# A ring of their own for the fp32 experts' weights, and one pair of PSUM banks for an fp32 step

## The chip, the core and the metric

The kernel runs on one core of a Trainium2 chip. The time is in device microseconds of one execution, as the median of several runs; lower is better. Durations in the profile come from one profiled execution.

## What is computed

One layer of a diffusion transformer on 1024 tokens of width 1024: a mixer of two kinds of attention, and behind it a mixture of experts. All tensors are fp32. The change touches the experts alone:

```python
logits = (h @ w_router + b_router).astype(jnp.float32)
top_logits, top_e = lax.top_k(logits, TOP_K)          # 4 of 32 experts for each token
top_w = jax.nn.softmax(top_logits, axis=-1).astype(h.dtype)
...
def expert_block(args):
    xe, e = args
    gu = xe @ w_gu[e] + b_gu[e]                       # 1024 -> 2048
    x_glu = jnp.minimum(gu[:, :D_FF], SWIGLU_LIMIT)
    x_lin = jnp.clip(gu[:, D_FF:], -SWIGLU_LIMIT, SWIGLU_LIMIT)
    act = (x_lin + 1) * (x_glu * jax.nn.sigmoid(SWIGLU_ALPHA * x_glu))
    return act @ w_dn[e] + b_dn[e]                    # 1024 -> 1024
```

Each token's result is the sum of its four experts' outputs, weighted by `top_w`. The weights of all 32 experts, 12 MB each, have to be read once.

## The kernel before

The phases ahead of the experts (mixer, router, slot tables) end near 1150 us of the profile. `moe` then works through the 32 experts, ordered by their number of tokens: expert of rank r gets `CAPS[r]` slots, 304 for the first and 56 for the last; tokens beyond that go to an overflow part. By its slots an expert has one of three modes:

- T (16 experts, 136 to 304 slots): weights are the stationary operand, tokens the moving one, the result is transposed. Products run in fp32r on a split: a weight piece `raw` of 128 x 1024 becomes `hi` (a rounded copy, ScalarE, L1518) and `lo` (`raw - hi`, VectorE, L1529). TensorE adds `hi` times both halves of the tokens (L1701) and `lo` times the upper half (L1702); above 256 slots there are three products (L1704 to L1706).
- N (9 experts, 128 slots): tokens are stationary, the same split of weights (L1669 to L1671).
- F (7 experts, 56 to 96 slots): plain fp32 products from `raw`, without a split (L1698). Each matmul uses 64 columns of the array; the two halves `a = 0, 64` write the two halves of the partitions.

The places p = 0 to 31 alternate: even places hold the T experts from the widest on, places 1 to 13 the F experts, and odd places from 15 on the N experts. An expert has six steps: four of kind U (j = 0 to 3, a quarter of gate and up columns each) and two of kind D (half of the output columns each). A step takes four pieces (q = 0 to 3), each with two of the eight blocks of the contraction. The list `steps` alternates the two experts of a pair step by step, so T and F (later T and N) steps follow each other all along.

The order on each engine is written out by the program, in the order in which Python issues the instructions. Within a step, `tra` (T and F) or `nat` (N) issues the matmuls of a quarter and then calls `slot(p)`. A slot advances the generators in `chains` (the work that follows a step: activation functions, splits of activations, and from `hot` and `cold` the transposes of tokens, which are started in T and N slots only), then issues up to two splits and up to two loads of later pieces. There is one ring of 8 `raw` pieces for all modes, 7 `hi` and 6 `lo`. A split is not issued until its load is three slots old. The raw buffer of an F piece comes free when TensorE has read it, that of another piece when VectorE has made its `lo`. All weight loads are issued by SP, one after the other (L1497): one that waits for its buffer holds back those behind it.

PSUM has a ring of three tiles `g5`, each of two banks (`gps`, 3 buffers). A T step or an F step takes two of them (`pss` in `tra`, one for each half `gi`), an N step one. They are emptied after the step: in a wide U step by ScalarE's bias (L1762) and VectorE's add (L1768), in a wide D step by L1836 and L1845, in F steps and the two widest T by VectorE's L1776 (U) and ScalarE's L1836 (D). `evac` issues ScalarE's part at the end of q = 3, the chain issues VectorE's part in the slot at the end of the step, behind the splits of the slots before.

Of the kernel before, what the change touches and what calls it, by code (L numbers as in the profile page):

```python
# [18 lines left out]
P = 128  # L19
# [1420 lines left out]
class Moe2(Tail):  # L1440
    def moe(self):
# [6 lines left out]
        N_HI, N_LO, N_RAW = 7, 6, 8  # L1448
# [4 lines left out]
        lop = self.pool(es, "lo5", N_LO)  # L1453
        es = ExitStack()
# [29 lines left out]
        st = {"l": 0, "h": 0, "s": 0, "out": 0, "c": 0, "n": -9}  # L1484
        at = {}
        whole = lambda i: mode[pieces[i][1]] == "F"

        def load(n=1, eng="sync"):
            for _ in range(n):
                o = st["l"] - N_RAW  # L1490
                if st["l"] >= len(pieces) or o >= st["c"] and whole(o):
                    return
                k, p, j, q = pieces[st["l"]]
                e = ereg(eng, p)
                r = rawp.tile([P, 1024], F32, name="raw5")
                src = A["w_gu" if k == "U" else "w_dn"]
                getattr(nc, eng).dma_start(r, src[ds(e, 1), j * 4 + q].rearrange("a p c -> p (a c)"))  # L1497
                if whole(st["l"]):
                    his[pieces[st["l"]]] = r
                else:  # L1500
                    raws[st["l"]] = r
                at[st["l"]] = st["n"]
                st["l"] += 1

        def split_hi(n=1, now=False):
            for _ in range(n):
                while st["h"] < len(pieces) and whole(st["h"]):
                    st["h"] += 1
                i = st["h"]
                if i >= len(pieces):  # L1510
                    return
                if i >= st["l"]:
                    load(i + 1 - st["l"])
                if i >= st["l"] or at[i] > st["n"] - 3 > -3 and not now:
                    return
                st["out"] += 1
                his[pieces[i]] = hi = hip.tile([P, 1024], F32R, name="hi5")
                ACT.activation(hi, raws[i], AF.Copy)  # L1518
                st["h"] += 1

        def split_lo(n=1):
            for _ in range(n):
                while st["s"] < len(pieces) and whole(st["s"]):
                    st["s"] += 1
# [3 lines left out]
                los[pieces[i]] = lo = lop.tile([P, 1024], F32R, name="lo5")  # L1528
# [149 lines left out]
        def tra(key, x, p, evac):  # L1678
# [6 lines left out]
            for q in range(4):  # L1685
# [26 lines left out]
                if q < 3:  # L1712
                    slot(p)
# [391 lines left out]
```

## Time and profile before

| | |
|---|---|
| median of 3 runs | 2846.4 us (2839.77 to 2849.7) |
| profiled execution | 2844.65 us, span 2842.8 us |
| first T matmul of an expert, first F step, first N step | 1182, 1211, 1978 us |
| last matmul of an expert | 2799 us |
| PE busy over the span | 2646.8 us (93%) |
| DVE, ACT busy | 1747.6 us (61%), 1409.9 us (50%) |
| splits | 600 `hi` at 1052 ns, 600 `lo` at 1222 ns |
| weight loads of the experts | 768 of 512 KB |

The part to look at lies between 1182 and 2799 us. A group of instructions is named by its line, engine, tiles (out<-in) and count; behind the bar stand its busy time, the mean of one, and the idle time of the engine just before it with what ended it. "PE g L1698 <- DVE gx L1768" says that a matmul of line 1698 that writes a tile `g` waited until the VectorE instruction of line 1768 was done. Matmuls are pipelined and their ends are modelled, so the length of a step is read from its start to the start of the next.

### The profile page before, as it was taken

How to read it: one execution, taken by the hardware profiler on the slowest of the kernel's cores; microseconds unless marked ns; L12 is line 12 of the kernel's file. 1: busy time of each engine (PE TensorE's matmuls, PEld its weight loads, DVE VectorE, ACT ScalarE, POOL GpSimd, SP SyncE). 2: the span in 40 equal slices, each digit the busy share in tenths (PEclk: the TensorE clock that was granted, in tenths of full speed). 3: DMA queues.
4: the chain of work that ended last, by engine and by line, in shares of the span. 5: the costliest groups of instructions: out<-in, count | busy, mean ns of one | idle time of the engine just before them, and what ended most of it. 6: DMA issues, size and time to landing. Idle time of an engine off the chain costs nothing. (4 is left out here: it accounts for less than half of the span.)

```text
span 2842.8 us, 52306 instructions
## 1 busy us (share of the span) xinstructions
PE 2646.8 (93%) x19986; PEld 2251.9 (79%) x19986; DVE 1747.6 (61%) x3001; ACT 1409.9 (50%) x2334; POOL 557.1 (20%) x485
## 2 busy tenths in 40 slices
PE   6999999999999999599988999999999999999993
PEld 3788887555688778599978888998889888988883
DVE  3722322767788456454454554555888888888885
ACT  3421212555677235334334444445676777777774
POOL 2310001656543313201011011011001100110001
PEclk8999999999999999699999999999999999999997
DMA  6224551502232443567687687787889888998886
GB/s 234 72 94 176 185 196 45 159 23 41 49 73 48 156 150 113 195 209 252 230 268 251 239 281 249 258 290 262 279 288 306 289 283 298 311 307 281 301 300 235
DMA packets 197422, 588.15 MB, mean 207 GB/s; under 512 B 50400, under 2 KB 57136, under 8 KB 197024
## 3 DMA queue, kind: packets, MB, share of 16 engines
q1 hardware_dynamic: 174432, 521.51, 53.5%
q0 software_dynamic: 19152, 61.86, 8.2%
q8 instruction: 158, 2.59, 0.4%
q10 hardware_dynamic: 3584, 1.40, 0.2%
q14 instruction: 96, 0.79, 0.1%
HBM read 527.92 MB, written 58.08 MB: 206 GB/s over the span
## 5 line engine op out<-in xcount | busy, mean ns | idle before, releaser
L1529 DVE TENSOR_TENSOR lo<-raw,hi 128x1024 fp32r<-128x1024 f32 x600 | 722.4, 1222 | 405.6 <-ACT hi L1518 395.6
L1518 ACT ACTIVATE hi<-raw 128x1024 fp32r<-128x1024 f32 x600 | 611.0, 1052 | 59.8 <-DMA raw<-in_w_gu_dram 40.5
L1701 PE MATMUL g<-xT,hi 128*128 128x320 f32 (+10 forms) x1792 | 524.3, 334 | 10.6 <-DVE gx L1776 7.7
L1702 PE MATMUL g<-xT,lo 128*128 128x256 f32 x1792 | 483.5, 280 | 0.0
L1701 PEld LDWEIGHTS g<-xT,hi 128*128 128x128 f32 x1792 | 337.1, 188 | 26.6 <-issue 10.2
L1702 PEld LDWEIGHTS g<-xT,lo 128*128 128x128 f32 x1792 | 337.6, 188 | 1.5
L1870 POOL DMA_INDIRECT f_d<-y,slot x34 | 55.3, 1627 | 1252.8 <-ACT y L1858 1127.1
L1701 PE MATMUL g<-aT,hi 128*128 128x288 f32 (+10 forms) x896 | 264.9, 336 | 4.8 <-DVE gx L1776 4.8
L1702 PE MATMUL g<-aT,lo 128*128 128x256 f32 x896 | 242.4, 281 | 0.0
L1701 PEld LDWEIGHTS g<-aT,hi 128*128 128x128 f32 x896 | 169.1, 189 | 12.0 <-issue 6.1
L174 DVE TENSOR_TENSOR wlo<-raw,whi 128x1024 fp32r<-128x1024 f32 x33 | 42.1, 1289 | 219.4 <-ACT whi L173 219.2
L1702 PEld LDWEIGHTS g<-aT,lo 128*128 128x128 f32 x896 | 169.4, 189 | 0.4
L1698 PE MATMUL g<-xN,raw 128*64 128x88 f32 (+5 forms) x3584 | 136.1, 237 | 20.8 <-DVE gx L1768 12.2
L1698 PEld LDWEIGHTS g<-xN,raw 128*64 128x64 f32 x3584 | 129.8, 140 | 27.7 <-DVE gx L1768 13.0
L859 ACT ACTIVATE p<-S 128x512 f32<-128x512 f32 x160 | 94.2, 596 | 103.8 <-PE S L858 99.0
L613 DVE TENSOR_REDUCE mn<-S 128x1 f32<-128x512 f32 x180 | 100.8, 594 | 66.3 <-PE S L612 66.0
L400 PE MATMUL mm<-hTh,whi 128*128 128x512 f32 (+1 forms) x416 | 123.9, 385 | 1.7 <-ACT whi L173 1.7
L400 PE MATMUL mm<-hTh,wlo 128*128 128x512 f32 (+1 forms) x416 | 123.2, 384 | 0.0
L400 PE MATMUL mm<-hTl,whi 128*128 128x512 f32 (+1 forms) x416 | 123.1, 383 | 0.0
L1669 PE MATMUL g<-hi,xN 128*128 128x512 f32 x288 | 117.5, 408 | 0.0
L1671 PE MATMUL g<-lo,xN 128*128 128x512 f32 x288 | 113.7, 395 | 0.0
L1670 PE MATMUL g<-hi,xN 128*128 128x512 f32 x288 | 113.7, 395 | 0.0
(415 smaller groups left out, 5735.4 us busy)
## 6 DMA issues: line engine op xcount, KB each, us to landing
raw<-in_w_gu_dram SPq DMA_DIRECT2D x512, 512.0 KB, 5.9
raw<-in_w_dn_dram SPq DMA_DIRECT2D x256, 512.0 KB, 4.6
raw<-in_w_mod_dram SPq DMA_DIRECT2D x40, 512.0 KB, 4.3
raw<-in_w_in_dram SPq DMA_DIRECT2D x34, 512.0 KB, 4.7
x<-in_x_dram SPq DMA_DIRECT2D x16, 512.0 KB, 5.0
sig_d<-stg POOLq DMA_DIRECT2D x16, 512.0 KB, 2.9
sig<-sig_d SPq DMA_DIRECT2D x8, 1024.0 KB, 4.9
kraw<-ka_d SPq DMA_DIRECT2D x16, 320.0 KB, 6.9
```

The source lines that it names most:

```text
L400: T.matmul(ps[:, :n], w[:, ks], h[:, k, a:a + n], start=k == 0 and pi == 0, stop=k == KT - 1 and pi == 2)
L613: nc.vector.tensor_reduce(out=u.mn[:, i, j:j + 1], in_=ps[:, :n], op=ALU.min, axis=AX.X)
L859: nc.scalar.activation(u.p[t // 2][:, t % 2 * 512:t % 2 * 512 + 512], ps, AF.Exp, scale=-1.0)
L1518: ACT.activation(hi, raws[i], AF.Copy)
L1529: V.tensor_tensor(out=lo, in0=raws.pop(i), in1=f(his[pieces[i]]), op=ALU.subtract)
L1669: T.matmul(ps[:m], x[:, kk, P:P + m], hi[:, cs], start=False, stop=False)
L1670: T.matmul(ps[:m], x[:, kk, :m], hi[:, cs], start=False, stop=False)
L1671: T.matmul(ps[:m], x[:, kk, :m], lo[:, cs], start=False, stop=kk == 7)
L1698: T.matmul(ps[a:a + 64, :c], hi[:, cs.start + a:cs.start + a + 64], x[:, kk, :], start=first, stop=last)
L1701: T.matmul(ps[:, :2 * c], hi[:, cs], x[:, kk, :], start=first, stop=False)
L1702: T.matmul(ps[:, :256], lo[:, cs], x[:, kk, :256], start=False, stop=last)
L1870: G.indirect_dma_start(out=self.f_d, out_offset=bass.IndirectOffsetOnAxis(ap=SL[p][xi][:n, 0:1], axis=0), in_=Y[p][xi][:n], in_offset=None ...
```

## The change

Five things change in `moe`.

1. F pieces get a ring of their own, `rawf`, of four buffers, one step's worth. `load_whole` fills it: a new function `few` calls it after each piece's last use in an F step, so a step's four pieces are loaded in the second half of the F step before. The ring of the others shrinks from 8 to 6 `raw`, 7 to 6 `hi`, 6 to 5 `lo`; the sum stays 21 pieces.
2. `few` takes the place of `tra` for F. It takes one PSUM tile (two banks, each with two parts of 256 columns) instead of two, and runs over the four pieces twice: r = 0 and r = 1 for the two parts of a bank. The count of matmuls is the same.
3. Slots of F steps advance chains but issue no split and no load. In slots of T and N steps both splits go ahead while fewer than five pieces are split beyond the ones used (`st["c"]` counts pieces of T and N only). The rule of three slots and `ready` are gone.
4. `load` takes T and N pieces only, up to six beyond the last `lo`.
5. When the last F step is done, the four buffers of `rawf` become two more `hi` and two more `lo`; the limit rises to eight `hi` and seven `lo`.

At the end of the program two of the eight loads of the residual go to `hi` buffers instead of `raw` ones.

On TensorE, the third F step of place 9 (88 slots) and the T step D of place 8 after it. `g5` are PSUM tiles, `raw5` and `rawf` weight pieces. Before:

```order
L1702 MATMUL g5_16071<-xT_14947,lo5_15975 128x256
L1698 MATMUL g5_16182<-xN_15461,raw5_15997 64x88 x8
L1698 MATMUL g5_16183<-xN_15461,raw5_15997 64x88 x8
L1698 MATMUL g5_16182<-xN_15461,raw5_16017 64x88 x8
L1698 MATMUL g5_16183<-xN_15461,raw5_16017 64x88 x8
L1698 MATMUL g5_16182<-xN_15461,raw5_16036 64x88 x8
L1698 MATMUL g5_16183<-xN_15461,raw5_16036 64x88 x8
L1698 MATMUL g5_16182<-xN_15461,raw5_16062 64x88 x8
L1698 MATMUL g5_16183<-xN_15461,raw5_16062 64x88 x8
L1701 MATMUL g5_16275<-aT_15462,hi5_16126 128x432
L1702 MATMUL g5_16275<-aT_15462,lo5_16128 128x256
```

and now:

```order
L1693 MATMUL g5_16060<-xT_14948,lo5_15937 128x256
L1717 MATMUL g5_16177<-xN_15453,rawf_16018 64x88 x8
L1717 MATMUL g5_16177<-xN_15453,rawf_16028 64x88 x8
L1717 MATMUL g5_16177<-xN_15453,rawf_16039 64x88 x8
L1717 MATMUL g5_16177<-xN_15453,rawf_16049 64x88 x8
L1717 MATMUL g5_16177<-xN_15453,rawf_16018 64x88 x8
L1717 MATMUL g5_16177<-xN_15453,rawf_16028 64x88 x8
L1717 MATMUL g5_16177<-xN_15453,rawf_16039 64x88 x8
L1717 MATMUL g5_16177<-xN_15453,rawf_16049 64x88 x8
L1692 MATMUL g5_16263<-aT_15454,hi5_15967 128x432
L1693 MATMUL g5_16263<-aT_15454,lo5_15969 128x256
```

Eight rows of eight matmuls as before. The two tiles have become one, and each piece is read twice, four groups apart.

On VectorE around the end of the T step before this F step (its PSUM tiles are read by the two adds into `gx` that are 2x216 wide). Before:

```order
L1786 SCALAR_TENSOR_TENSOR aN_15785<-gx_16055,gs_16088 128x2x88
L1529 TENSOR_TENSOR lo5_16128<-raw5_16064,hi5_16126 128x1024
L1529 TENSOR_TENSOR lo5_16132<-raw5_16066,hi5_16130 128x1024
L1768 TENSOR_TENSOR gx_16142<-g5_16070,gx_16142 128x2x216
L1770 TENSOR_SCALAR gx_16142<-gx_16142 128x2x216
L1768 TENSOR_TENSOR gx_16153<-g5_16071,gx_16153 128x2x216
L1772 TENSOR_SCALAR gx_16153<-gx_16153 128x2x216
L1529 TENSOR_TENSOR lo5_16162<-raw5_16068,hi5_16160 128x1024
L1529 TENSOR_TENSOR lo5_16166<-raw5_16090,hi5_16164 128x1024
L1784 TENSOR_TENSOR gs_16200<-gs_16200,gx_16142 128x2x216
L1786 SCALAR_TENSOR_TENSOR gx_16142<-gx_16153,gs_16200 128x2x216
L1793 TENSOR_TENSOR aT_15462<-gx_16142,aT_15462 128x2x216
```

and now:

```order
L1532 TENSOR_TENSOR lo5_16105<-raw5_15780,hi5_16103 128x1024
L1532 TENSOR_TENSOR lo5_16127<-raw5_15893,hi5_16125 128x1024
L1779 TENSOR_TENSOR gx_16139<-g5_16059,gx_16139 128x2x216
L1781 TENSOR_SCALAR gx_16139<-gx_16139 128x2x216
L1779 TENSOR_TENSOR gx_16150<-g5_16060,gx_16150 128x2x216
L1783 TENSOR_SCALAR gx_16150<-gx_16150 128x2x216
L1532 TENSOR_TENSOR lo5_16159<-raw5_15917,hi5_16157 128x1024
L1795 TENSOR_TENSOR gs_16194<-gs_16194,gx_16139 128x2x216
L1797 SCALAR_TENSOR_TENSOR gx_16139<-gx_16150,gs_16194 128x2x216
L1804 TENSOR_TENSOR aT_15454<-gx_16139,aT_15454 128x2x216
L1787 TENSOR_SCALAR gx_16255<-g5_16177,bcol_14223 128x88 x2
L1787 TENSOR_SCALAR gx_16256<-g5_16177,bcol_14223 128x88 x2
```

Before, two splits `lo` stand directly ahead of the adds and two behind them. Now each slot of the T step has one: the two ahead of the adds belong to the slots after its second and third quarter, the one behind to the slot at its end.

On SP, the loads ahead of the same F step (`raw5_15997`, `raw5_16017`, `raw5_16036`, `raw5_16062` before, `rawf_16018` to `rawf_16049` now). Each load has a row `ISA` of its own, which sets registers. Before:

```order
L1497 DMA raw5_15997<-in_w_gu_dram 128x1024
L1497 ISA
L1497 DMA raw5_16017<-in_w_gu_dram 128x1024
L1497 ISA
L1497 DMA raw5_16036<-in_w_gu_dram 128x1024
L1497 ISA
L1497 DMA raw5_16062<-in_w_gu_dram 128x1024
L1497 ISA
L1497 DMA raw5_16064<-in_w_dn_dram 128x1024
```

and now:

```order
L1496 DMA raw5_15971<-in_w_dn_dram 128x1024
L1496 ISA
L1496 DMA rawf_16018<-in_w_gu_dram 128x1024
L1496 ISA
L1496 DMA rawf_16028<-in_w_gu_dram 128x1024
L1496 ISA
L1496 DMA rawf_16039<-in_w_gu_dram 128x1024
L1496 ISA
L1496 DMA rawf_16049<-in_w_gu_dram 128x1024
L1496 ISA
L1496 DMA raw5_16083<-in_w_dn_dram 128x1024
```

Before, the F pieces stand between the loads of the T steps around them in the order of use. Now they stand between the last load of one T step and the first of the next.

The diff:

```diff
--- before.py
+++ after.py
@@ -1445,12 +1445,15 @@
         NE = 32
         CT = max(256, max(caps))
         CF = 96
-        N_HI, N_LO, N_RAW = 7, 6, 8
+        N_HI, N_LO, N_RAW, N_F = 6, 5, 6, 4
         es = self.early = ExitStack()
         bhl = self.pool(es, "bia").tile([P, 3072], F32R, name="bhl")
         rawp = self.pool(es, "raw5", N_RAW)
         hip = self.pool(es, "hi5", N_HI)
         lop = self.pool(es, "lo5", N_LO)
+
+        fctx = ExitStack()
+        more = {"f": self.pool(fctx, "rawf", N_F, side="right")}
         es = ExitStack()
         xgp = self.pool(es, "xg", 3)
         xtp = self.pool(es, "xt5", 1)
@@ -1481,52 +1484,52 @@
                       ("U", p + 1, 3), ("D", p, 1), ("D", p + 1, 0)] + nxt[:1] + [("D", p + 1, 1)] + nxt[1:]
         pieces = [(k, p, j, q) for k, p, j in steps for q in range(4)]
         raws, his, los = {}, {}, {}
-        st = {"l": 0, "h": 0, "s": 0, "out": 0, "c": 0, "n": -9}
-        at = {}
-        whole = lambda i: mode[pieces[i][1]] == "F"
-
-        def load(n=1, eng="sync"):
+        st = {"l": 0, "f": 0, "h": 0, "s": 0, "c": 0}
+        split = [x for x in pieces if mode[x[1]] != "F"]
+        whole = [x for x in pieces if mode[x[1]] == "F"]
+
+        def fetch(pool, name, x, eng="sync"):
+            k, p, j, q = x
+            e = ereg(eng, p)
+            r = pool.tile([P, 1024], F32, name=name)
+            src = A["w_gu" if k == "U" else "w_dn"]
+            getattr(nc, eng).dma_start(r, src[ds(e, 1), j * 4 + q].rearrange("a p c -> p (a c)"))
+            return r
+
+        def load(n=1):
             for _ in range(n):
-                o = st["l"] - N_RAW
-                if st["l"] >= len(pieces) or o >= st["c"] and whole(o):
+                if st["l"] < min(len(split), st["s"] + N_RAW):
+                    raws[st["l"]] = fetch(rawp, "raw5", split[st["l"]])
+                    st["l"] += 1
+
+        def load_whole(n=1):
+            for _ in range(n):
+                if st["f"] < len(whole):
+                    his[whole[st["f"]]] = fetch(more["f"], "rawf", whole[st["f"]])
+                    st["f"] += 1
+
+        def part(pool, name, i):
+
+            if name in more and i % 4 == 3:
+                pool = more[name]
+            return pool.tile([P, 1024], F32R, name=name)
+
+        def split_hi(n=1):
+            for _ in range(n):
+                i = st["h"]
+                if i >= min(len(split), st["l"]):
                     return
-                k, p, j, q = pieces[st["l"]]
-                e = ereg(eng, p)
-                r = rawp.tile([P, 1024], F32, name="raw5")
-                src = A["w_gu" if k == "U" else "w_dn"]
-                getattr(nc, eng).dma_start(r, src[ds(e, 1), j * 4 + q].rearrange("a p c -> p (a c)"))
-                if whole(st["l"]):
-                    his[pieces[st["l"]]] = r
-                else:
-                    raws[st["l"]] = r
-                at[st["l"]] = st["n"]
-                st["l"] += 1
-
-        def split_hi(n=1, now=False):
-            for _ in range(n):
-                while st["h"] < len(pieces) and whole(st["h"]):
-                    st["h"] += 1
-                i = st["h"]
-                if i >= len(pieces):
-                    return
-                if i >= st["l"]:
-                    load(i + 1 - st["l"])
-                if i >= st["l"] or at[i] > st["n"] - 3 > -3 and not now:
-                    return
-                st["out"] += 1
-                his[pieces[i]] = hi = hip.tile([P, 1024], F32R, name="hi5")
+                his[split[i]] = hi = part(hip, "hi5", i)
                 ACT.activation(hi, raws[i], AF.Copy)
                 st["h"] += 1
 
         def split_lo(n=1):
             for _ in range(n):
-                while st["s"] < len(pieces) and whole(st["s"]):
-                    st["s"] += 1
                 i = st["s"]
                 if i >= st["h"]:
                     return
-                los[pieces[i]] = lo = lop.tile([P, 1024], F32R, name="lo5")
-                V.tensor_tensor(out=lo, in0=raws.pop(i), in1=f(his[pieces[i]]), op=ALU.subtract)
+                los[split[i]] = lo = part(lop, "lo5", i)
+                V.tensor_tensor(out=lo, in0=raws.pop(i), in1=f(his[split[i]]), op=ALU.subtract)
                 st["s"] += 1
 
 
@@ -1588,20 +1591,15 @@
 
         def slot(p):
             advance(p)
-            st["n"] += 1
-            for most in (N_HI, N_HI - 1)[:1 if mode[p] == "F" else 2]:
-                if st["out"] < most:
+            if mode[p] == "F":
+                return
+            n = N_HI + 2 if "hi5" in more else N_HI - 1
+            for _ in range(2):
+                if st["h"] - st["c"] < n:
                     split_hi()
+                if st["s"] - st["c"] < n - 1 + ("hi5" not in more):
                     split_lo()
-            load()
-            if st["l"] < min(st["c"] + 11, st["s"] + N_RAW):
-                load()
-
...
@@ -1693,11 +1688,7 @@
                         for i in range(2):
                             ps = pss[gi][:, i]
                             cs = slice(k * 512 + (gi * 2 + i) * P, k * 512 + (gi * 2 + i) * P + P)
-                            if mode[p] == "F":
-                                for a in (0, 64):
-                                    T.matmul(ps[a:a + 64, :c], hi[:, cs.start + a:cs.start + a + 64], x[:, kk, :],
-                                             start=first, stop=last)
-                            elif wide:
+                            if wide:
                                 T.matmul(ps[:, :2 * c], hi[:, cs], x[:, kk, :], start=first, stop=False)
                                 T.matmul(ps[:, :256], lo[:, cs], x[:, kk, :256], start=False, stop=last)
                             else:
@@ -1706,11 +1697,31 @@
                                 T.matmul(ps[:, :c], lo[:, cs], x[:, kk, :c], start=False, stop=last)
                     if q == 3:
                         evac(gi, pss[gi])
-                if mode[p] == "T":
-                    st["out"] -= 1
                 st["c"] += 1
                 if q < 3:
                     slot(p)
+
+        def few(key, x, p, evac):
+
+            c = caps[posr[p]]
+            ps = gps.tile([P, 2, 512], F32, name="g5")
+            for r in range(2):
+                for q in range(4):
+                    wants(key, q)
+                    w = his[key + (q,)]
+                    for k in range(2):
+                        kk = q * 2 + k
+                        for i in range(2):
+                            for a in (0, 64):
+                                cs = k * 512 + (i * 2 + r) * P + a
+                                T.matmul(ps[a:a + 64, i, r * 256:r * 256 + c], w[:, cs:cs + 64], x[:, kk, :],
+                                         start=kk == 0, stop=kk == 7)
+                    if r:
+                        load_whole()
+                    if q % 2 and r + q < 4:
+                        slot(p)
+            for h in range(2):
+                evac(h, ps[:, h].rearrange("p (i c) -> p i c", i=2))
 
         def tokens_of(p, j, ps):
 
@@ -1793,7 +1804,7 @@
                 V.tensor_tensor(out=at[:, fs, c:2 * c], in0=xs, in1=f(at[:, fs, :c]), op=ALU.subtract)
                 todo["D", p, j] -= 1
 
-            tra(key, X[p], p, ev)
+            (tra if mode[p] == "T" else few)(key, X[p], p, ev)
             chains.append(chain())
             slot(p)
 
@@ -1861,7 +1872,7 @@
                 return
                 yield
 
-            tra(key, at, p, ev)
+            (tra if mode[p] == "T" else few)(key, at, p, ev)
             chains.append(chain())
             slot(p)
 
@@ -1910,7 +1921,8 @@
             advance()
         split_hi(N_HI - 4)
         split_lo(N_LO - 4)
-        st["n"] = 0
+        load(2)
+        load_whole(N_F)
         for k, p, j in steps:
             (step_U if k == "U" else step_D)(p, j)
             if (k, p, j) == ("U", 0, 0):
@@ -1922,6 +1934,10 @@
             for q in range(4):
                 his.pop((k, p, j, q))
                 los.pop((k, p, j, q), None)
+            if (k, p, j) == whole[-1][:3]:
+                fctx.close()
+                more.clear()
+                more.update({n: self.pool(self.early, n + "b", 2, side="right") for n in ("hi5", "lo5")})
         while hot or cold or chains:
             advance()
         es.close()
```

More of the change, by code (lines that the diff above doesn't have):

```diff
@@ L1590, in slot @@
             advance(p)
-            st["n"] += 1
-            for most in (N_HI, N_HI - 1)[:1 if mode[p] == "F" else 2]:
-                if st["out"] < most:
+            if mode[p] == "F":
[3 more added lines that the diff above has]
+                if st["h"] - st["c"] < n:
                     split_hi()
+                if st["s"] - st["c"] < n - 1 + ("hi5" not in more):
                     split_lo()
-            load()
-            if st["l"] < min(st["c"] + 11, st["s"] + N_RAW):
-                load()
-        def ready():
-            while st["s"] <= st["c"] and not whole(st["c"]):
-                split_hi(1, True)
-                split_lo()
+            load(2)
         def need(*keys):
@@ L1663, in nat @@
                 wants(key, q)
-                ready()
                 hi, lo = his[key + (q,)], los[key + (q,)]
@@ L1686, in tra @@
                 wants(key, q)
-                ready()
-                hi, lo = his[key + (q,)], los.get(key + (q,))
+                hi, lo = his[key + (q,)], los[key + (q,)]
                 for gi in range(2):
@@ L1708, in tra @@
                         evac(gi, pss[gi])
-                if mode[p] == "T":
-                    st["out"] -= 1
                 st["c"] += 1
@@ L1912, in moe @@
         split_lo(N_LO - 4)
-        st["n"] = 0
+        load(2)
+        load_whole(N_F)
         for k, p, j in steps:
```

## The prediction

> **What bounds the kernel now.** I began with the table of stages, cut at the starts of pairs of experts: one wide expert (T) beside one fp32 expert (F), and last a T beside an expert of 128 slots (N). Columns after the stretch: its length, the busy time of PE, PEld, DVE, ACT and POOL with counts, the granted clock, the DMA share, GB/s.
>
> ```profile
> 1211.37:1293.89 82.52, 78.85 (x1061) 76.72 (x1060) 40.30 (x72) 29.46 (x45) 0.93 (x1) 1.00 0.58 204
> 1407.81:1520.90 113.09, 101.73 (x1208) 89.81 (x1204) 56.34 (x89) 47.50 (x82) 10.05 (x7) 0.98 0.75 251
> 1737.95:1843.43 105.48, 96.78 (x1202) 93.06 (x1200) 53.63 (x88) 45.81 (x81) 9.39 (x6) 1.00 0.79 263
> 1843.43:1949.43 106.00, 99.83 (x1203) 96.01 (x1201) 53.37 (x89) 45.61 (x81) 9.17 (x7) 0.98 0.78 265
> 2051.45:2148.43 96.98, 95.82 (x584) 87.44 (x582) 81.09 (x108) 67.72 (x100) 10.62 (x7) 1.00 0.88 287
> ```
>
> In the T-N pair TensorE is busy for 95.82 of 96.98 us; that part is bound by PE and little is to be had there. In the T-F pairs PE idles 4 to 11 us of each, though DVE, ACT and the DMA engines are all less busy than in the T-N pair. So something makes PE wait there that is no throughput limit. The list of waits of PE alone names it, first from the first F step to the first N step (1211 to 1984 us), then from there to 2805 us (us in total, times, longest):
>
> ```profile
> PE g L1698 <- DVE gx L1768: 18.1, 11, 3.8
> PE g L1698 <- DVE yT L1845: 14.6, 10, 1.7
> PE g L1701 <- DVE gx L1776: 12.5, 13, 1.9
> PE g L1704 <- DVE gx L1776: 8.1, 5, 1.7
> PE g L1701 <- ACT gx L1836: 2.6, 3, 1.2
> PE g L1698 <- DVE gx L1776: 1.7, 2, 0.9
> PE g L1704 <- ACT gx L1836: 0.9, 1, 0.9
> ...
> PE t L1628 <- DVE xT L1615: 9.0, 8, 1.3
> PE t L1735 <- DVE gx L1729: 4.9, 9, 1.1
> ```
>
> The first seven rows are one wait: a matmul that writes the PSUM tile `g` is released by the instruction that empties an older `g` (the adds of L1768 and L1845, the F clamps of L1776, ACT's bias of L1836). Sum 58.5 us in 45 waits. In the T-N part no row has `g` at all. PE waits nowhere for a split weight (`hi`, `lo`) or for a weight's DMA. So the bound in the T-F pairs is the ring of three PSUM tiles: T and F take two each, so each step needs a tile that the step right before it has used.
>
> One such wait from the timeline, an F step after a T step that ended at 1515.26:
>
> ```profile
> 1513.15 2.00 ACT L1518 ACTIVATE hi<-raw 128x1024 fp32r<-128x1024 f32 x2
> 1514.24 2.36 DVE L1529 TENSOR_TENSOR lo<-raw,hi 128x1024 fp32r<-128x1024 f32 x2 [9.80 <-ACT hi L1518]
> 1515.26 0.72 PE L1698 MATMUL g<-aN,raw 128*64 128x72 f32 x16
> 1516.51 1.28 DVE L1845 TENSOR_TENSOR yT<-g,yT 128x512 f32<-128x512 f32 x2
> 1517.25 3.72 PE L1698 MATMUL g<-aN,raw 128*64 128x72 f32 x112 [1.28 <-DVE yT L1845]
> ...
> 1458.63 4.22 PE L1698 MATMUL g<-xN,raw 128*64 128x72 f32 x128
> ```
>
> DVE had idled 9.80 us, then got two splits at once just as T ended; the add that frees the bank stood behind them. The last row is the same size of F step without a wait. The disturbed one runs from 1515.26 to 1520.97, 5.71 us, against 4.22: it lost 1.49, of which 1.28 is the shown wait and 0.21 the restart of the pipeline.
>
> **The change, part by part.** *One PSUM tile for F.* The 64 matmuls of an F step stay, in pairs over the two column halves, with the same operands: cost 0. With T on two tiles and F on the third, each step gets tiles whose last user is two steps back: T has a whole F step for its emptying. How long that emptying takes, from a T step that ended at 1679.41, with the F step after it and the next F step:
>
> ```profile
> 1679.41 5.08 PE L1698 MATMUL g<-xN,raw 128*64 128x88 f32 x128
> 1695.66 5.08 PE L1698 MATMUL g<-xN,raw 128*64 128x88 f32 x128
> ...
> 1679.14 0.61 DVE L1768 TENSOR_TENSOR gx<-g,gx 128x432 f32<-128x432 f32 x1 [1.92 <-ACT gx L1762]
> 1680.39 0.61 DVE L1768 TENSOR_TENSOR gx<-g,gx 128x432 f32<-128x432 f32 x1 [0.22 <-ACT gx L1762]
> ...
> 1211.37 3.95 PE L1698 MATMUL g<-xN,raw 128*64 128x56 f32 x128
> ```
>
> The second add ends at 1681.00, 1.6 us after T. Even with two splits ahead (2.36) that is 4.0 us. The shortest F step lasts 3.95 and the usual one 5, and the second tile is wanted only after the first half of T's first quarter. So the cover is about 1 us or more everywhere, and the T-N part, with the same pattern of tiles, shows zero. I take the whole 58.5 us as removed, and the 45 restarts at 0.21, 9.5 us; bounds: 34 (half, if the cover fails) to 68. **-68.0.**
>
> *Splits in T steps only, a step ahead.* The count is the same: 600 `hi` at 1052 ns and 600 `lo` at 1222 ns.
>
> ```profile
> L1529 DVE TENSOR_TENSOR lo<-raw,hi 128x1024 fp32r<-128x1024 f32 x600 | 722.4, 1222 | 405.6 <-ACT hi L1518 395.6
> L1518 ACT ACTIVATE hi<-raw 128x1024 fp32r<-128x1024 f32 x600 | 611.0, 1052 | 59.8 <-DMA raw<-in_w_gu_dram 40.5
> ```
>
> Four `lo` are 4.9 us of DVE in a T step of 11.2 (1695.66 less 1679.41 less 5.08), one per quarter. A `lo` now reuses the buffer of the quarter just finished, so DVE waits in order for PE, at most until that quarter ends; behind it stand the chains of earlier steps, which nobody on PE needs within a quarter. T always begins with five pieces split. Cost 0. If that lead were gone, each quarter would wait for `hi` and `lo`, 2.3 us; nothing in the order makes that so.
>
> *F's own ring.* The step's four loads move from anywhere in the shared ring to the second half of the F step before, each behind PE's last read of its buffer. A piece is free after 5/8 of the F step (quarter 0) and first needed at the next one's start: 5.08 x 3/8 + 11.2 = 13.1 us, the same for the others, less 1 to 2 us in which SP first issues T's last load, which waits for a `lo`. So 11 to 12 us are left. The DMA view of the two parts (median us from issue to landing at the end; queue rows: packets, MB, share), first 1211 to 1984, then 1984 to 2805:
>
> ```profile
> raw<-in_w_gu_dram SPq DMA_DIRECT2D x226, 512.0 KB, 7.2
> q0 software_dynamic: 5378, 17.69, 10.2%
> ...
> raw<-in_w_gu_dram SPq DMA_DIRECT2D x266, 512.0 KB, 5.4
> ```
>
> 7.2 us fits into 11. Four pieces at once is a smaller burst than the eight that SP now issues. The pair of 105.48 us at 263 GB/s shortened by 10 us needs 290, and the T-N pair moves 287 without a PE wait. A median says nothing of the tail, so I estimate one F step in eight late by 1 us: **+5**, bounds 0 and 98 (below).
>
> [...]
>
> *Start and end.* PE's wait for the first gathered rows is
>
> ```profile
> PE t L1628 <- DMA xg<-h_d,slot: 21.4, 2, 19.8
> ```
>
> and ten pieces instead of twelve are requested before these rows. Two pieces at 287 GB/s are 3.7 us; the gather hangs on its slot table as well, so I take **-2**, bounds 0 and -3.7. The four F loads come after it. At the end, two of the eight loads of the residual go into `hi` buffers, read by PE before the last steps. The T-N part gets 8 `hi`, 7 `lo`, 6 raw for 7, 6, 8: its 14 us of `t` waits may shrink or not; 0, bounds -14 and +5.
>
> **Sum.** The profiled execution took 2844.65 (span 2842.8 and 1.85 around it), 1.75 below the median of 2846.4. 2844.65 - 68.0 + 5 - 2 = 2779.7, say **2780 us**.
>
> **The rivals.** *F weights a little late.* Landing of about 12 us against 11 to 12 of slack, 0.8 us on 41 F steps, gives back 33: 2779.7 - 5 + 33 = 2808. For it: the lumps of four behind PE; against it: 7.2 us.
>
> *F weights late on every step: slower.* The ring has no fifth buffer, so nothing is loaded earlier. If landing doubles to 14.4, each F step waits 2.4 us after 12 of slack: 41 x 2.4 = 98, and 2844.65 - 68 - 2 + 98 = 2873. It decides from 70 / 41 = 1.7 us per step, a landing of 13.7. Against it: DMA share 0.78 now, and 0.88 carried next door.
>
> *The emptying is still late.* T's add stays behind a split and F is too short to hide it: half of the waits stay, 2844.65 - 34 - 2 = 2809. Against it: the T-N part.
>
> *More than the sum.* The T-N part loses its 14 us of `t` waits as well and no F piece is late: 2844.65 - 68 - 2 - 14 = 2761.
>
> **How the numbers follow.** Forecast 0.68; a little late 0.10; emptying still late 0.07; more than the sum 0.06; a loss of F weights that just eats the gain 0.04; late on every step 0.05. A change under 0.3% (8.5 us) can't be told from none. Faster is the first four cases, 0.91; same 0.04; slower 0.05. The range 2764 to 2809 takes in the forecast with its own bounds (F lateness 0 to 25 us, start and T-N part some us either way), the two partial cases at 2808 and 2809, and the near half of the best one.
>
> **What would show it.** Right: after, the T-F part has no row of PE waiting for `g`, all F steps of one size last the same, DVE's splits stand singly in the quarters of T, and the T-F pairs shrink by 4 to 12 us each with a DMA share near 0.85. The T-N part keeps its length within 5 us. Wrong: PE rows that wait for a DMA into `rawf`, or `g` rows released by L1768's or L1845's counterpart; or F steps longer than 5.08 at 88 columns without a wait, which would mean that the new order of matmuls costs by itself.

## The result and the profile after

The changed kernel takes 2764.89 us (median of 4 runs, 2762.26 to 2767.21), the kernel before beside it 2844.53 (2839.77 to 2849.7): a ratio of 0.9719, 95% interval 0.9698 to 0.974. A second set beside the last experiment gave 2758.18 (5 runs) against 2841.24, 0.9705 (0.969 to 0.9721). The profiled execution has a span of 2761.6 us, 81.2 less than the 2842.8 of before.

The table of stages, first of before, cut at its first F step, first N step and last matmul of an expert. Columns: window, length, busy time and count of PE, PEld, DVE, ACT, POOL, granted clock, DMA share, GB/s:

```profile
1211.37:1978.16 766.79, 707.72 (x8746) 671.30 (x8745) 378.91 (x618) 319.51 (x539) 62.65 (x45) 0.99 0.75 252
1978.16:2799.20 821.04, 806.79 (x5088) 728.56 (x5086) 694.50 (x938) 583.65 (x875) 79.21 (x57) 1.00 0.88 296
```

and of after, the same two parts and then the four T-F pairs that the prediction showed:

```profile
1210.78:1906.16 695.38, 693.11 (x8745) 665.79 (x8745) 386.64 (x619) 321.44 (x539) 60.87 (x45) 1.00 0.83 277
1906.16:2714.80 808.64, 802.66 (x5088) 729.13 (x5086) 693.27 (x936) 589.90 (x874) 82.34 (x56) 1.00 0.89 298
...
1210.78:1289.66 78.88, 78.54 (x1062) 76.79 (x1061) 42.24 (x73) 29.13 (x43) 0.93 (x1) 1.00 0.64 221
1395.60:1494.60 99.00, 98.80 (x1208) 88.48 (x1204) 56.70 (x88) 47.67 (x81) 9.92 (x7) 1.00 0.84 283
1688.08:1783.12 95.04, 95.04 (x1203) 92.95 (x1201) 54.22 (x88) 46.04 (x80) 8.65 (x6) 1.00 0.87 293
1783.12:1879.45 96.33, 96.33 (x1202) 94.22 (x1200) 54.30 (x89) 45.79 (x80) 7.97 (x7) 1.00 0.85 290
```

The T-F part lost 71.4 us and PE is now busy for 693.11 of its 695.38 us, with the same count of instructions. The T-N part lost 12.4. The start (to the first F step) moved by -0.6, the tail behind the last matmul of an expert by +3.2 (43.6 to 46.8). Together: -81.2. The four T-F pairs shrank by 3.6 to 14.1 us, where the prediction had said 4 to 12. The twelve F steps of 88 columns now last 5.00 to 5.15 us each, from their start to the start of the next step; before, they took 5.0 to 8.2.

PE's waits of after from the first expert to the end (the four longest rows), and one F step with its neighbour of the same size:

```profile
PE t L1746 <- DVE gx L1740: 4.2, 5, 1.5
PE t L1626 <- DVE xT L1613: 1.6, 7, 0.3
PE g L1717 <- issue: 0.8, 1, 0.8
PE g L1717 <- DMA rawf<-in_w_gu_dram: 0.7, 2, 0.5
```

```profile
1630.05 1.23 DVE L1532 TENSOR_TENSOR lo<-raw,hi 128x1024 fp32r<-128x1024 f32 x1 [0.65 <-PE g L1693]
1632.56 1.23 DVE L1532 TENSOR_TENSOR lo<-raw,hi 128x1024 fp32r<-128x1024 f32 x1 [1.28 <-PE g L1693]
1634.62 0.61 DVE L1779 TENSOR_TENSOR gx<-g,gx 128x432 f32<-128x432 f32 x1 [0.83 <-ACT gx L1773]
1634.90 5.07 PE L1717 MATMUL g<-xN,rawf 128*64 128x88 f32 x128
1635.87 0.61 DVE L1779 TENSOR_TENSOR gx<-g,gx 128x432 f32<-128x432 f32 x1 [0.22 <-ACT gx L1773]
```

The 45 waits of `g` for an emptied tile (58.5 us) are gone, without one left over; 1.5 us in three waits for `rawf` or issue stand in their place. T's second add still ends 1.6 us after T (1636.48), but nothing of PE hangs on it: the F step starts at once and the next T step starts on time.

One thing was in the trace of before that the prediction had not read. The table of stages of before, cut at three short windows:

```profile
1485.10:1488.51 3.41, 3.41 (x14) 3.03 (x13) 0.72 (x2) 0.60 (x1) 0.00 (x0) 0.50 0.86 352
1553.40:1560.23 6.83, 4.92 (x74) 4.92 (x76) 6.60 (x10) 3.97 (x9) 0.00 (x0) 0.50 0.93 295
1925.41:1928.82 3.41, 3.41 (x46) 3.41 (x46) 2.83 (x4) 0.66 (x1) 0.00 (x0) 0.50 0.84 233
```

The clock granted to TensorE was 0.50 for 3.4, 6.8 and 3.4 us. The first stretch begins 1.0 us after a wait of 1.9 us, the second 1.9 us into one of 3.8 us, the third 0.2 us after one of 1.5 us. After has no such stretch between 1190 and 2640 us. In the first of them a matmul of L1701 (512 columns) with its one of L1702 (256 columns) takes 0.64 us, from start to start; right behind it, at a clock of 1.00, 0.35. Half of the busy time in them (3.41, 4.92 and 3.41) is 5.9 us, an estimate of what they cost. So the -71.4 closes nearly: 58.5 of waits, 9.5 of restarts (an estimate, 45 times the 0.21 us of the prediction's one step), 5.9 of half clock, less the 1.5 of new waits, 72.4.

### The profile page after: what moved, and what is told of

It reads as the page before. It is cut to its first block, busy times and chain, and to the rows that moved or that the text cites. A ratio compares the mean times of both kernels' runs of the same rounds, so it can differ in the third digit from the quotient of the medians.

```text
span 2761.6 us, 52451 instructions
## 1 busy us (share of the span) xinstructions
PE 2627.6 (95%) x19986; PEld 2246.1 (81%) x19986; DVE 1754.1 (64%) x3001; ACT 1419.0 (51%) x2334; POOL 560.7 (20%) x485
## 5 line engine op out<-in xcount | busy, mean ns | idle before, releaser
L1523 ACT ACTIVATE hi<-raw 128x1024 fp32r<-128x1024 f32 x600 | 626.4, 1054 | 130.5 <-PE g L1692 59.7
L1881 POOL DMA_INDIRECT f_d<-y,slot x34 | 62.5, 1838 | 1206.0 <-ACT y L1869 1062.7
L1717 PE MATMUL g<-xN,rawf 128*64 128x88 f32 (+5 forms) x3584 | 131.5, 234 | 1.8 <-issue 0.8
L1717 PEld LDWEIGHTS g<-xN,rawf 128*64 128x64 f32 x3584 | 125.9, 137 | 7.7 <-issue 5.6
```

The source lines that it names most:

```text
L1717: T.matmul(ps[a:a + 64, i, r * 256:r * 256 + c], w[:, cs:cs + 64], x[:, kk, :], start=kk == 0, stop=kk == 7)
L1881: G.indirect_dma_start(out=self.f_d, out_offset=bass.IndirectOffsetOnAxis(ap=SL[p][xi][:n, 0:1], axis=0), in_=Y[p][xi][:n], in_offset=None ...
```

## The experiments

All of these compute the full result. The table gives the stages of each profiled execution (start to the first F step; T-F part; T-N part; tail) and the ratio to the kernel before with its interval. The medians come from four sets, in which the kernel before took 2839.76 to 2846.32 us, so kernels of different sets are compared by their ratios. "Lump" is experiment 4, "start and end" 6, "shared ring, late buffers" 7.

| | start | T-F | T-N | tail | median | ratio |
|---|---|---|---|---|---|---|
| before | 1211.4 | 766.8 | 821.1 | 43.6 | 2844.53 | 1 |
| after | 1210.8 | 695.4 | 808.6 | 46.8 | 2764.89 | 0.9719 (0.9698 to 0.974) |
| after, second set | 1205.6 | 696.6 | 807.0 | 47.9 | 2758.18 | 0.9705 (0.969 to 0.9721) |
| F on two tiles | 1209.3 | 717.6 | 807.1 | 47.1 | 2785.1 | 0.9812 (0.9794 to 0.983) |
| one tile only | 1207.4 | 694.2 | 824.6 | 44.5 | 2770.75 | 0.9752 (0.9734 to 0.977) |
| no late buffers | 1208.8 | 699.8 | 824.3 | 47.2 | 2782.09 | 0.9781 (0.9765 to 0.9797) |
| splits in one lump | 1209.6 | 707.8 | 806.5 | 47.4 | 2777.62 | 0.979 (0.9768 to 0.9812) |
| lump, F on two tiles | 1210.9 | 842.6 | 807.5 | 47.2 | 2909.31 | 1.0244 (1.0227 to 1.0261) |
| F loads later | 1205.1 | 985.5 | 808.0 | 47.5 | 3050.33 | 1.0719 (1.0698 to 1.074) |
| start and end | 1206.4 | 700.7 | 806.7 | 43.8 | 2765.29 | 0.9727 (0.9712 to 0.9742) |
| shared ring, late buffers | 1211.9 | 693.4 | 812.4 | 43.8 | 2765.41 | 0.9731 (0.9718 to 0.9744) |

My theory: the one PSUM tile brings the gain. Rivals: the new rule of splits, the own ring, or the late buffers bring it.

**1. F back on two PSUM tiles, all else changed.**

```diff
-            ps = gps.tile([P, 2, 512], F32, name="g5")
+            pss = [gps.tile([P, 2, 512], F32, name="g5") for _ in range(2)]
...
-                                T.matmul(ps[a:a + 64, i, r * 256:r * 256 + c], w[:, cs:cs + 64], x[:, kk, :],
+                                T.matmul(pss[i][a:a + 64, r, :c], w[:, cs:cs + 64], x[:, kk, :],
...
-                evac(h, ps[:, h].rearrange("p (i c) -> p i c", i=2))
+                evac(h, pss[h])
```

> The changed kernel, but an F step takes two PSUM tiles again (one for each bank index i); own ring and steady splits stay. Theory 'tiles' (the waits come from the rotation of three tiles): every F step now needs the first tile of the T step just ended, whose add came 0.3 us after T's end where no split stood before it, so about 0.3 us of wait and 0.2 of restart on 42 F steps, 20 us: 2785 us, and rows of PE waiting for g at the F line, released by VectorE's add. Rival 'splits' (the waits come from pairs of splits that stand ahead of the adds; steady splits alone cure them): 2765 to 2768, no such rows over 3 us.

Measured: 2785.1. The waits for an emptied tile are back, at a quarter of their old size (PE's waits from the first expert on):

```profile
PE g L1717 <- DVE yT L1856: 7.6, 10, 1.0
PE g L1717 <- DVE gx L1779: 4.1, 7, 0.9
...
PE g L1695 <- DVE gx L1787: 2.9, 6, 0.5
PE g L1692 <- DVE gx L1787: 1.8, 3, 0.8
```

16.4 us of `g` in 26 waits, none over 1.0, and no half clock. So with F on two tiles the rest of the change shortens these waits. The new rule of splits puts one `lo` ahead of the adds where there had been two; but F's own ring and its two passes over the pieces are in this run as well, and it does not tell them apart. Experiment 4 does for the place of the splits.

**2. One PSUM tile alone, in the kernel before** (its shared ring of 8, its rule of splits): the function `few` and its two calls.

```diff
+        def few(key, x, p, evac):
...
+                    if r:
+                        st["c"] += 1
...
-            tra(key, X[p], p, ev)
+            (tra if mode[p] == "T" else few)(key, X[p], p, ev)
...
-            tra(key, at, p, ev)
+            (tra if mode[p] == "T" else few)(key, at, p, ev)
```

> The kernel before, with its shared ring and its rule for splits, but an F step takes one PSUM tile and runs over its pieces twice. Theory 'tiles': the 58 us of waits for g go, the 12 us that the T-N part lost stay: 2844.5 - 68 = 2777 us, up to 2785. Rival 'splits': the waits stay for the most part, 2820 to 2844 us.

Measured: 2770.75, below the 2777 to 2785 of the theory "tiles", with a T-F part of 694.2 us, no longer than after's 695.4. PE's waits from the first expert on:

```profile
PE t L1628 <- DVE xT L1615: 9.0, 8, 1.3
PE t L1757 <- DVE gx L1751: 7.0, 9, 3.3
PE g L1701 <- DVE gx L1790: 2.9, 2, 1.7
```

The one tile gives the whole gain of the T-F part, but for two waits of `g` (2.9 us): the own ring and the splits a step ahead add nothing to it that shows. The T-N part stays at 824.6.

**3. The four late buffers left out**: the T-N part works with 6 `hi`, 5 `lo`, 6 raw and the new rule, whose limit stays at five pieces ahead.

```diff
-                more.update({n: self.pool(self.early, n + "b", 2, side="right") for n in ("hi5", "lo5")})
```

> The changed kernel without its last part: after the last F step the four buffers of rawf stay unused, the limit stays at five pieces ahead with 6 hi, 5 lo and 6 raw. Theory 'rule' (the 12 us that the T-N part gained come from the splits that no longer wait for the quarter to come): the same time, 2763 to 2768 us. Rival 'buffers' (they come from the 8 hi and 7 lo): the T-N part returns to its old length or longer, 2777 us or more.

Measured: 2782.09; the T-N part is back at 824.3. What the buffers do there is seen on DVE and ACT. The largest wait of each in the T-N part, in the list of waits by engine of before:

```profile
ACT aN L1612 <- PE t L1735: 71.8, 36, 3.2
...
DVE lo L1529 <- ACT hi L1518: 106.0, 145, 2.3
```

of this experiment:

```profile
ACT aN L1610 <- PE t L1746: 71.4, 36, 3.2
...
DVE lo L1532 <- ACT hi L1523: 109.7, 147, 2.3
```

and of after:

```profile
ACT aN L1610 <- PE t L1746: 47.2, 36, 1.6
...
DVE lo L1532 <- ACT hi L1523: 17.1, 31, 1.3
```

With 5 or 6 `lo` and 6 or 7 `hi`, DVE stands at almost every `lo` until its `hi` is done (145 waits, 106 us). With two more of each `hi` is mostly ahead of it (31 waits, 17.1 us). A `lo` then waits for other things as well, for the buffer that PE reads among them: all waits ahead of a `lo` together fall from 110.1 to 68.5 us. So the DVE instructions behind a `lo`, the transposed tokens `xT` and the activations `gx` among them, come earlier, and PE's 13.9 us of `t` waits become 5.8; in this experiment they are 16.7. Of the other 4.3 us of the 12.4, 4.1 lie in PE's busy time (806.79 to 802.66); I did not follow them further.

**4. The splits of a T step in one lump of four**, in the slot after the third quarter, on one tile and on two (experiment 1's edit added).

```diff
-            for _ in range(2):
+            for _ in range(2 if "f" not in more else 4 if st["c"] % 4 == 3 else 0):
...
-            load(2)
+            load(2 if "f" not in more else 4)
```

> The changed kernel, but in the T-F part all four splits of a T step stand in the slot after its third quarter, right ahead of the adds that empty PSUM; F keeps one tile. Four lo take 4.9 us from the third quarter's end, so the adds come some 2.2 to 3.5 us after T's end. Theory 'tiles': an F step of 3.9 to 5.4 us hides that, 2765 to 2772 us. Rival 'splits': waits for g come back, 0.5 to 1.5 us on each of some 80 steps, 2800 us or more.

> Both undone in the T-F part: four splits right ahead of the adds and two PSUM tiles for F. Both theories: F waits 2.2 us or more for the first add on 42 steps, about 100 us: 2860 us, more than the kernel before if the clump of four is worse than its pairs. If the two parts only add up, the loss is that of the two runs with one part each; if the tiles decide when the splits matter, it is far more than their sum.

Measured: 2777.62 and 2909.31, the first between what the two theories expected, the second dearer than the 2860 of both. With one tile the lump costs 12.4 us in the T-F part, and PE waits for other things than the splits, with 6.8 us of half clock behind two of these waits:

```profile
PE g L1717 <- DMA rawf<-in_w_gu_dram: 9.8, 10, 2.2
...
PE g L1692 <- DVE yT L1856: 0.2, 1, 0.2
```

With two tiles the same lump costs 125 more than two tiles without it. Its waits, then one of them in the timeline, then the clock in it:

```profile
PE g L1717 <- DVE gx L1779: 42.1, 11, 4.3
PE g L1717 <- DVE yT L1856: 41.7, 10, 4.4
PE g L1717 <- DVE gx L1787: 8.0, 3, 3.5
PE g L1717 <- ACT yT L1847: 4.2, 3, 2.1
...
1619.78 4.63 DVE L1532 TENSOR_TENSOR lo<-raw,hi 128x1024 fp32r<-128x1024 f32 x4 [3.61 <-ACT hi L1523]
1620.98 0.36 PE L1717 MATMUL g<-xN,rawf 128*64 128x80 f32 x4
1624.93 1.14 DVE L1856 TENSOR_TENSOR yT<-g,yT 128x448 f32<-128x448 f32 x2
1625.60 7.28 PE L1717 MATMUL g<-xN,rawf 128*64 128x80 f32 x124 [4.26 <-DVE yT L1856]
...
1624.60:1631.43 6.83, 5.83 (x88) 5.84 (x90) 1.90 (x4) 0.00 (x0) 0.00 (x0) 0.50 0.55 205
```

The add stands behind four `lo`, F's second tile is the one it empties, and PE stops for 4.26 us; the rest of the F step runs at half clock for 5.8 us. The waits sum to 96.0 us. The trace has 116.1 us at 0.50, in which PE is busy for 100.3; half of that, by the estimate above, is 50. Together 146, restarts not counted, against 147.2 measured (842.6 - 695.4). So the two edits are not additive: one at a time they cost 22.2 and 12.4 us of the T-F part, together 147.2. The one tile is what makes the place of the splits harmless. What the lump still costs with it is waits for `rawf`; the edit also issues T's loads in lumps, and that these make F's late is argued, since no run lumped the splits alone.

**5. F loads issued later**, after the second quarter of the T step between, 5.6 us ahead of the F step where the change has about 13.

```diff
-                    if r:
-                        load_whole()
...
+                if q == 1:
+                    load_whole(st["w"] + 4 - st["f"])
```

> The changed kernel, but the four loads of the next F step are issued after the second quarter of the T step between, not in the second half of the F step before: half a T step, 5 to 6 us, is left until the first use, where the change leaves 11 to 12. It prices the rival 'F weights late'. If a piece takes 7.2 us to land, as the median of the kernel before, each F step waits 1.5 to 2 us: 41 x 1.7 = 70 us, 2835. If it lands in 4 to 5 us, as the loads at the start of the T-F part, nearly nothing waits: 2765 to 2775 us.

Measured: 3050.33, far outside what either theory expected. PE's waits, and a stretch of 200 us in the T-F part:

```profile
PE g L1719 <- DMA rawf<-in_w_gu_dram: 95.1, 79, 4.2
PE g L1719 <- DMA rawf<-in_w_dn_dram: 73.3, 43, 3.6
...
1600.00:1800.00 200.00, 152.00 (x1629) 140.73 (x1631) 76.26 (x121) 62.65 (x108) 11.61 (x9) 0.85 0.60 199
```

168.4 us of waits, 4.0 for each of the 42 F steps, and a clock of 0.85 in the stretch. Between 1190 and 2640 us the clock stands at 0.50 for 252.6 us, in which PE is busy for 192.6; half of that, by the same estimate, is 96. The sum is 265 of the 290.1 measured (985.5 - 695.4); smaller rows of PE's waits hold 11.0 more, and the rest, with the restarts, was not taken apart. So the lead of the change is needed. It also gives an estimate of how much is to spare: 5.6 us of lead left 4.0 missing, so a step's four pieces want some 9.6, against the 13.1 less 1 to 2 that they have in the change, 1.5 to 2.5 us spare. That is little: in after's first profile PE waited 0.7 us for `rawf`, in the second 4.5, without the late buffers 3.3, with the lump 9.8.

**6. Start and end**: slot tables and the gather ahead of the first splits, and the final adds all on VectorE.

```diff
-                (nc.gpsimd if i in (1, 3, 5) else V).tensor_tensor(out=fs[i], in0=fs[i], in1=xs[i], op=ALU.add)
+                V.tensor_tensor(out=fs[i], in0=fs[i], in1=xs[i], op=ALU.add)
...
+        slots(0, "scalar")
+        slots(1, "scalar")
...
-            if i == 2:
-                slots(0, "scalar")
+            if i == 0:
                 gather(0)
-                slots(1, "scalar")
```

> The changed kernel with two edits outside the change: the slot tables and the gather of the first expert are issued ahead of the first splits, and at the end VectorE does all final adds, where GpSimd did three. Expected: PE's wait of 19.9 us for the first gathered rows shrinks by about 3 us, since ScalarE issued the tables 5 us after it could; at the end a VectorE multiply takes 3.3 us beside GpSimd's add and 1.3 us alone, so two tiles take 5.1 us instead of 6.2: 3 us in all. Sum -6: 2759 us. If the transfers of the last tiles bound the end, only the first part shows: 2762.

Measured: 2765.29, a ratio not to be told from after's; neither 2759 nor 2762 came. The tail is 3.0 us shorter than after's in the profile. The start is 4.4 shorter, but the second set of the unchanged kernel after shows 1205.6 without any edit there. The T-F part, which the edits do not touch, is 5.3 longer. Four profiles have the same code there (after twice, experiments 3 and 6): 695.4, 696.6, 699.8 and 700.7 us, with 1.5, 4.5, 4.0 and 5.2 us of waits for `rawf` or issue. A few us of difference in this part say nothing.

**7. The parts that carry, put together**: the kernel before with one tile (experiment 2), its shared ring of 8 up to the last F step, then 6 raw, 8 `hi`, 7 `lo` and the new rule, and the edits of experiment 6; beside it, after once more.

```diff
+        more = {"raw5": self.pool(fctx, "rawx", 2, side="right")}
...
+            if "hi5" in more:
+                for _ in range(2):
+                    if st["h"] - st["c"] < 8:
+                        split_hi(1, True)
+                    if st["s"] - st["c"] < 7:
+                        split_lo()
+                load(2)
+                return
...
+                more.update({n: self.pool(self.early, n + "b", 1, side="right") for n in ("hi5", "lo5")})
```

> The kernel before with one PSUM tile for F steps, its ring of eight raw shared by all modes and its rule of splits, up to the last F step; from then on the buffers and the rule of the changed kernel (6 raw, 8 hi, 7 lo); slot tables and gather ahead of the first splits; all final adds on VectorE. Nothing is left out. Theory 'three parts add' (one PSUM tile, late buffers and the two ends are independent, F's own ring and splits in T steps bring nothing): start to first F step 1206, T-F part 694, T-N part 807, tail 44, together 2751 of the profile and 2752 to 2757 timed, 8 to 13 us below the changed kernel. Rival 'own ring carries something': the T-F part is 3 to 6 us longer than 695, or F steps wait for DMA into raw, and the time is 2760 to 2770, no different from the changed kernel. Rival 'handover': the T-N part stays near 820, since the buffers regrouped at the last F step come too late for it, 2765 to 2770.

> The changed kernel again, beside the next one. Expected 2765, ratio 0.972, T-F part near 695 us, T-N part near 809, tail near 47. If the ring of four F buffers is late now and then, PE shows some us of waits for a DMA into rawf in this profile, where the first one had none.

Measured: 2765.41 against 2758.18 for after, whose stages came out near what was expected; its waits for `rawf` are 4.5 us (the first profile had 0.7, not none as the expectation has it). The theory that the parts add fell: it wanted 8 to 13 us below after, and the time is 7.2 above. The T-F part is the shortest of all (693.4) and the tail is 4.1 shorter than after's beside it, but the T-N part takes 812.4 against 807.0. The rows of PE's waits in its T-N part name the place:

```profile
PE t L1774 <- DVE gx L1768: 6.1, 5, 3.9
PE t L1645 <- DVE xT L1632: 0.8, 3, 0.3
```

One wait of 3.9 us falls into the second T step after the buffers change hands (place 14, 4.66 us longer than in after, with half clock for 3.4 us behind it); the rest of the part is the same within 1 us. "One tile only", which hands no buffers over, has a wait of 3.3 us for the same kind of `gx` in the same step, so the handing over is not its cause. Both kernels have the shared ring and the old rule of splits up to the last F step. That with the changed kernel the split pieces are a step ahead when the T-N part begins is argued, not shown, and no run tells the ring from the rule.

From the first F step on, the two kernels take 1549.6 and 1551.5 us, no difference. In the profiles the new one loses 6.3 us ahead of that (1211.9 against 1205.6), in spite of the edits that were to shorten the start; why is open.

## Why the prediction was right, by its steps

The forecast was 2780. The measured 2764.89 lies only 0.9 us inside the low end of the range, and the second set's 2758.18 lies below it, so that the range held is partly luck. The mechanism of the likeliest case is the one that the runs show; the profile lost 81.2 us where the prediction's terms add up to 65.0, most of the difference in the T-N part. The rival "more than the sum", 2761, came nearer in the number. Of its two conditions, that no F piece is late holds nearly (1.5 us), and of the 14 us of `t` waits that it let go, 8.1 went.

- **One PSUM tile for F, -68.0**: right, -71.4 in the T-F part. All 45 waits went, with their restarts. Missing from the term were the 5.9 us, by the estimate above, of the half clock in and behind three of the waits. Experiments 1 and 2 show the cause from both sides: the tile alone gives all of the T-F gain, and without it 22 us of it are lost. That the cover of "about 1 us or more" holds even when four `lo` stand ahead of the adds is shown by the lump on one tile: 0.2 us of such waits.
- **Splits in T steps only, 0**: right for this kernel (experiment 2 against after). It is not nothing where F takes two tiles: there the `g` waits are 16.4 us with the rest of the change, the rule among it, 58.5 without, and 96.0 with the splits in lumps. The tile and the rule cover the same loss.
- **F's own ring, +5**: 1.5 to 5.2 us of waits in the four profiles with this code; right in size, and experiment 5 bears out that the slack over landing is a few us. The T-F part of the two kernels with the shared ring, 694.2 and 693.4 us, is no longer. The median landing of these loads in the second profile of after is the 7.2 us that I had taken from before, the row of DMA issues:

```profile
rawf<-in_w_gu_dram SPq DMA_DIRECT2D x112, 512.0 KB, 7.2
```

  In before the gate and up pieces landed in 7.2 us in the T-F part and in 5.4 in the T-N part. The queue of the gathers and scatters (`q0`) does not account for it: it has 10.2% of the engines' time in the T-F part of before and 10.4% in its T-N part. In the T-F part of this second profile the gate and up pieces of T land in 4.2 us beside the 7.2 of F; T's are issued singly or in pairs, F's four in a row.

- **Start, -2**: cannot be told. The first F step began anywhere from 1205.1 to 1211.9 us in the profiles here, and at 1210.8 and 1205.6 for the same kernel.
- **T-N part, 0, bounds -14 to +5**: this is the step that was mis-sized, -12.4 measured, and the line "the T-N part keeps its length within 5 us" was wrong. I had taken "bound by PE" from one pair with 95.82 of 96.98 us busy and left its 13.9 us of `t` waits where they were. Experiment 3 shows that the late buffers removed them, by letting `hi` run ahead of `lo`. The row that could have told it before was DVE's, `lo` waiting for `hi` 145 times in this part.
- **End, 0**: mis-sized by 3.2. Two of the residual's loads go to `hi` buffers and no longer wait for a split, and all eight are issued by 2708, 6.8 us before the last matmul of an expert, where it was 5.3 before. SP's and GpSimd's rows of after at the end:

```profile
2697.50 9.52 SPq L1951 DMA_DIRECT2D raw<-x_d  x6
2707.07 0.90 SPq L1951 DMA_DIRECT2D hi<-x_d  x2
...
2705.32 2.39 POOL L1881 DMA_INDIRECT f_d<-y,slot  x1 [64.96 <-ACT y L1869]
2716.41 1.35 POOL L1881 DMA_INDIRECT f_d<-y,slot  x1 [8.71 <-ACTq L1355]
```

  and of before:

```profile
2779.82 14.06 SPq L1935 DMA_DIRECT2D raw<-x_d  x8
...
2789.77 1.55 POOL L1870 DMA_INDIRECT f_d<-y,slot  x1 [66.22 <-ACT y L1858]
2798.00 1.35 POOL L1870 DMA_INDIRECT f_d<-y,slot  x1 [6.67 <-issue]
```

  The second of these scatters starts 11.1 us after the first where it had been 8.2, and the chain at the end hangs on the last. That the 4 MB of loads cause it is argued from the order; no run moved them alone, and in experiment 3 they are issued later than in before and the tail is 47.2 all the same. So the cause is open. "One tile only", which loads them as before, has a tail of 44.5; experiment 6 shortens the tail to 43.8 by other means.
- **The rival "F weights late on every step"** had its mechanism right, as experiment 5 shows, and its price too low: 98 us for 2.4 us per step, where 4.0 per step cost 290. It counted the wait and not the clock behind it.

## What to carry to other kernels

Where PE waits for the emptying of a PSUM tile, count how many steps lie between a tile's last use and its next one: a step that fits its result into fewer tiles lets the work that empties them be late for nothing, as long as the step between is longer than the delay (here four splits, 4.9 us, begun before the end of T, beside steps of 3.9 to 5.4 us), and then the order of that work hardly matters. Look in the trace whether the clock falls behind a wait of PE, and if it does, price the wait by its length and by half of the busy time at half clock: here this gave 146 of the 147.2 us of the lump on two tiles, and 265 of the 290.1 of the late F loads. A part that is "bound by PE" still gives up its last per cent where an engine in program order stands behind another one's split: buffers by which the first can run ahead were worth 12 to 16 us here.

## What was unexpected in the hardware

The long waits of PE cost more than their length here. In the ten profiles other than experiment 5's, between 1190 and 2640 us, a granted clock of 0.50 began within all 21 waits of PE of 3.5 us and over or at most 1 us behind them, and lasted for 3.4 or 6.8 us. The same holds, up to 2 us behind, for 6 of the 9 waits between 2 and 3.5 us, and for 5 of the 89 between 0.8 and 2 us. By half of the busy time this made about 50 us of the 147 lost by the lump on two tiles, and 96 of the 290 of the late F loads.

The three stretches of before last 3.41, 6.83 and 3.41 us. The second begins 68.3 us behind the first and the third 372.0 us behind the second, 20 and 109 times 3.413 us. The 3.41 us ahead of each stretch of before:

```profile
1481.69:1485.10 3.41, 1.51 (x9) 1.08 (x9) 2.65 (x9) 0.95 (x2) 0.00 (x0) 1.00 0.90 344
1549.99:1553.40 3.41, 1.48 (x22) 1.07 (x20) 1.14 (x1) 2.05 (x3) 1.73 (x2) 0.99 1.04 338
1922.00:1925.41 3.41, 1.91 (x28) 1.47 (x28) 3.41 (x5) 3.41 (x8) 0.00 (x0) 1.00 0.42 121
```

PE was busy for 43 to 56% of them and idle for 1.5 to 1.9 us. In the ten profiles PE was busy for at most 56% of the 3.41 us ahead of each of the 31 stretches. A few stretches as idle kept the full clock behind them, in before the one that ends at 1771.8 (42% busy, with a clock of 1.00 in the 3.4 us behind it), so no sharp limit is shown.
